# Three FFN heads written out by hand on four engines, in a four-layer trunk on one core

## The chip, the core and the metric

The kernel runs on one core of a Trainium2 chip. A core has TensorE (PE, the matrix engine, with a weight-load side that the profile calls PEld), VectorE (DVE), ScalarE (ACT), GpSimd (POOL) and SyncE (SP, which here only issues DMAs); each takes its instructions from its own queue, in order, and engines wait for each other by semaphores. SBUF is the on-chip memory, PSUM the accumulators of PE. The metric is the device time of one execution, in microseconds (us); lower is better.

## The reference

A trunk of four layers on 512 tokens with D = 1024, everything in float32. Layer by layer the mixer is S5 (a diagonal state-space scan), GLA (gated linear attention), differential attention, and S5 again; behind each mixer stands a SwiGLU feed-forward network with 2816 hidden columns:

```python
for layer in range(DEPTH):
    h = rmsnorm(x, norm_mix[layer])
    mix = s5_mixer | gla_mixer | diff_attn_mixer     # by layer % 3
    x = x + mix
    h = rmsnorm(x, norm_ffn[layer])
    g, u = split(h @ w_gate_up[layer], 2)            # 1024 x 5632
    x = x + (silu(g) * u) @ w_down[layer]            # 2816 x 1024
return rmsnorm(x, norm_final)
```

## The kernel before

**Three matmuls for one.** A float32 operand is split into a high half (rounded to the format fp32r) and the low rest; a product is three matmuls, high x high, high x low, low x high. A split of a weight tile is `halves()`: ACT writes the high half (L235), DVE subtracts it from the weight for the low one (L236). Weights come by `staged()` into a ring of three buffers (`wst`, DMA issued by SP); split weights lie in a ring of five (`whl`).

**Seven products for eight.** The FFNs of layers 1, 2 and 3 (heads 1, 2 and 3 below) use a scheme of Strassen's kind. The left matrix, h transposed, is cut into quarters a11, a12, a21, a22 (tile `halves`, written by `keep`). From them `Sides` makes seven left sides: "11" and "12" are the split quarters themselves; "1" is s = a21 - a22, "2" is s - a11, "4" is s + a12, all three made in place in a21's room; "3" is a11 - a21; "22" is a22. `parts()` splits a side into halves (ACT L154, DVE L155); the totals are L177. The weight columns are cut into 11 blocks of 256 hidden columns; a block needs seven weights, some of them sums, and does seven products (`seven_product`, L458, 24 matmuls of 128x256 each): "one" (side 11), "two" (side 12), "five" (side 1), "six" (side 2), "seven" (side 3), "three" (side 4) and "four" (side 22). "one", "six", "seven" and "four" add up in one PSUM bank, "five" and "three" in a second; "two" has one of its own (PSUM: four banks `acc`, two `s`).

**Where weights lie.** A block's weights "11" and "3" are staged; "21", "1" and "22" lie in rooms (`slots`: three of their own, two lent from a buffer of the activations, and, when the sides are built, the four quarters and the gain's tile). "1" and "3" are sums of two quarters of the weight: SP loads the one, and POOL issues a DMA that adds the other onto it (L485). Within a block W["1"] is then changed twice by a DVE add: plus W["22"] ahead of "six" (L530), plus W["21"] ahead of "four" (L546).

**The norm.** h is x times the gain, without the row's factor. That factor (`finish`: squares on ACT, mean on DVE, the power on POOL, L118) is applied to the products: `rows()` writes four diagonal matrices on DVE (L125), spreads them over the partitions by four matmuls with a matrix of ones on PE (L128, tile `rows`), and ACT copies the result to `R`; `scaled` uses R in `gate1` and `four`.

**The order.** A tile scheduler puts the instructions of each engine into an order, from the program's order, costs and priorities, unless a `manual_schedule` names the engine: then the program's order is kept. In the GLA and the differential-attention mixers PE is kept in program order. At an FFN's head only SP is, for the first loads:

```python
with self.tc.manual_schedule(engines={mybir.EngineType.SP}):
    f[0]["roomed"](None, lent[:, 0])
    f[0]["direct"]()
    f[1]["direct"]()
    f[0]["summed"]()
```

**The tail and the head.** The mixer's last product is `gemm_b` with a `tail`: its last four k-steps run row tile by row tile (t = 0 to 3), so that x is updated (L389), multiplied by the gain (`take`, L83), transposed by PE (`put`, L101) and kept (L158) tile by tile. The differential attention has a loop of its own for that. What I call the head is the part of `ffn()` from there on: block 0's and block 1's first products, the sides, the norm, up to the loop over groups of blocks (4, 4, 3). In that loop a group of blocks is done, and then its part of the down projection.

Of the kernel before, what the change touches and what calls it, by code (L numbers as in the profile page):

```python
# [60 lines left out]
class Left:  # L61
# [4 lines left out]
    def __init__(self, tr, grow, g=None):  # L66
# [10 lines left out]
    def take(self, t, d):  # L77
# [8 lines left out]
        tr.flush(1 - d)  # L86
        tr.pend.append(lambda: self.put(t, d, h))
# [20 lines left out]
    def finish(self):  # L108
# [4 lines left out]
        for t in range(NT):  # L113
            self.square(t, 1)
# [5 lines left out]
    def rows(self):  # L120
        tr = self.tr
        nc = tr.nc
        diag = tr.np_.tile([P, NT, P], F32, tag="h", name="diag")
        for t in range(NT):
            nc.vector.tensor_scalar(diag[:, t], tr.ident[:], self.r[:, t : t + 1], None, op0=ALU.mult)  # L125
        p = tr.tp("rows")
        for t in range(NT):
            nc.tensor.matmul(p[:, t], tr.ones[:], diag[:, t], start=True, stop=True)  # L128
        self.R = tr.np_.tile([P, SEQ], F32, tag="R", name="R", bufs=1)
        nc.scalar.copy(self.R[:].rearrange("p (a b) -> p a b", b=P), p[:])  # L130


class Sides(Left):

    def room(self):
# [3 lines left out]
        self.place = {"11": two[:, 0], "12": two[:, 1]}  # L141

    def open(self, pool):

        for n in ("3", "1", "2", "4", "22"):
            self.place[n] = pool.tile([P, 2, 4, 256], F32R, name="side" + n)
# [14 lines left out]

    def side(self, name):

        v = self.tr.nc.vector
        a11, a12, a21, a22 = (self.F[k] for k in ((0, 0), (0, 1), (1, 0), (1, 1)))
        s = a21
        if name == "22":
            self.parts("22", a22)
        elif name == "3":
            for k in (0, 2):  # L170
                ks = slice(k, k + 2)
                u = self.tr.np_.tile([P, 2, 256], F32, tag="h", name="s3")
                v.tensor_tensor(u[:], a11[:, ks], a21[:, ks], op=ALU.subtract)
                self.parts("3", u[:], ks)
        else:
            x, y, op = {"1": (a21, a22, ALU.subtract), "2": (s, a11, ALU.subtract), "4": (s, a12, ALU.add)}[name]
            v.tensor_tensor(s, x, y, op=op)  # L177
            self.parts(name, s)


class Trunk:
    def __init__(self, ctx, tc, ins, out):
# [23 lines left out]
        self.pend = []  # L206

# [46 lines left out]
    def gemm_b(self, stat, w, nk, c0, evac, k0=0, tail=0, between=()):  # L254
# [53 lines left out]
    def gemm_a4(self, left, hls, banks):  # L308

        for n, (hl, bank) in enumerate(zip(hls, banks)):  # L310
# [4 lines left out]
            if n == 3:  # L315
                left.rows()
# [132 lines left out]
    def seven_product(self, side, w, bank, first):  # L449

        hl = self.halves(w, 4, 256)
# [11 lines left out]
    def seven_block(self, fp, slots, left, wgu, b, turn):  # L463
# [6 lines left out]
        W, bank, keep, lent = {}, {}, {}, set()  # L470

        def load(name, q, half, plus=None, room=None):
            cut = lambda q, half: wgu[
                q * 512 : (q + 1) * 512, half * FFN_HIDDEN + b * 256 : half * FFN_HIDDEN + (b + 1) * 256
            ].rearrange("(a p) n -> p a n", p=P)
            if name in ("11", "3"):
                W[name] = self.staged(cut(q, half), 4, 256)
            else:
# [3 lines left out]
                nc.sync.dma_start(W[name][:], cut(q, half))  # L482
            w = W[name]
            if plus:
                self.added = nc.gpsimd.dma_start(w[:], cut(*plus), accum_op=ALU.add)  # L485
# [22 lines left out]

        def one():
            bank["a"] = self.acc("a")  # L510
            self.seven_product(A["11"], W["11"], bank["a"], True)
# [3 lines left out]
        def two():  # L515
            d = self.sbank("d")
            self.seven_product(A["12"], W["21"], d, True)
            v.tensor_tensor(keep["r1"][:], keep["r1"][:], d[:], op=ALU.add)
# [4 lines left out]
        def five():  # L523
            bank["c"] = self.acc("c")
            self.seven_product(A["1"], W["1"], bank["c"], True)
            keep["r5"] = T("r5")
            nc.scalar.copy(keep["r5"][:], bank["c"][:])

        def six():
            v.tensor_tensor(W["1"][:], W["1"][:], W["22"][:], op=ALU.add)  # L530
            self.seven_product(A["2"], W["1"], bank["a"], False)
# [13 lines left out]
        def four():  # L545
            v.tensor_tensor(W["1"][:], W["1"][:], W["21"][:], op=ALU.add)  # L546
# [20 lines left out]
            direct=direct, roomed=roomed, summed=summed, one=one, two=two, gate1=gate1, five=five, six=six, seven=seven,  # L567
            three=three, four=four,
        )

    def ffn(self, l, left, after=None, turn=False, aside=None):
# [5 lines left out]
        with self.tc.tile_pool(name=f"ffn{l}", bufs=1, reuse_waits="tile") as fp:  # L577
            left.open(fp)
            slots = [fp.tile([P, 4, 256], F32, name=f"slot{n}") for n in range(SLOTS)]
            self.jobs = aside(fp) if aside else iter(())  # L580
# [3 lines left out]
            lent = fp.tile([P, 2, 4, 256], F32, tag="act", name="lent", bufs=4)  # L584
# [11 lines left out]
            left.finish()  # L596
            f[0]["two"]()
            left.side("1")
            f[1]["two"]()
            left.side("2")  # L600
            f[0]["five"]()
            left.rows()
            f[0]["six"]()
            left.side("4")
            left.side("22")
            slots += left.freed() + [left.g[:].rearrange("p (k n) -> p k n", n=256)]
            b0 = 0
            for nb in (4, 4, 3):
                acts = []
                for n in range(b0, b0 + nb):  # L610
# [9 lines left out]
                    todo = ["one", "five", "six", "two", "gate1", "seven", "three"]  # L620
                    if n < 2:
                        todo = ["five", "six", "seven", "gate1", "three"][2 if n == 0 else 0 :]
# [694 lines left out]
    def s5_glu(self, L, zT, accs, after):  # L1317
# [4 lines left out]
        nxt = (Sides if L else Left)(self, after)  # L1322
        with self.tc.tile_pool(name=f"s5g_{L}", bufs=1) as p:
            for d in range(2):
# [18 lines left out]
                self.gemm_b(stat, wg, KT, d * 512, evac_a, tail=4 if d else 0)  # L1343
# [3 lines left out]
    def gla(self, l, left, after):  # L1347
# [4 lines left out]
        with self.tc.tile_pool(name="gla", bufs=1) as p, self.tc.manual_schedule(engines={mybir.EngineType.PE}):  # L1352
# [196 lines left out]
            nxt = Sides(self, after, g)  # L1549
            late = [lambda: turned(1, (0, 1)), lambda: turned(1, (2, 3))]  # L1550
            for d in range(2):
                self.gemm_b(so, wo, KT, d * 512, self.add_x(d, nxt), tail=4 if d else 0, between=late if d == 0 else ())
# [54 lines left out]
    def diff(self, l, left, after):  # L1607
# [3 lines left out]
        with self.tc.tile_pool(name="diff", bufs=1) as p, self.tc.manual_schedule(engines={mybir.EngineType.PE}):  # L1611
            T = lambda tag, bufs=2: p.tile([P, 512], F32, tag=tag, name=tag, bufs=bufs)
            mask = p.tile([P, NT, SEQ], BF16, name="mask")
# [28 lines left out]
            oT = [p.tile([P, 2, 4, SEQ], F32R, name="oT0"), None]  # L1642
# [6 lines left out]
            qks = [None, None]  # L1649
# [16 lines left out]
            def project(hf, z):  # L1666
                if z == 0:
                    qks[hf] = p.tile([P, 2, 4, SEQ], F32, tag="qk", name="qk", bufs=2)
# [150 lines left out]
            def evac0(t, ps):  # L1819
                if not nxt:  # L1820
                    nxt.append(Sides(self, after, gains[0]))
# [49 lines left out]
            run(last)  # L1871
            evac = self.add_x(1, nxt[0])
# [72 lines left out]
```

## Time and profile before

| | |
|---|---|
| three runs | 2402.25, 2408.87, 2411.74 us; median 2408.87 |
| the profiled execution | 2407.16 us, of which its span (the profile's axis) is 2405.4 us |
| busy share of the span | PE 95%, PEld 82%, DVE 62%, ACT 45%, POOL 12% |
| mean granted clock of PE | 0.976 of full speed |

Times in views are microseconds from the span's start. A group's row has its line, engine, operation, output and inputs by the program's names, shapes, and count; then busy time and mean ns of one, and the idle time of that engine just before it with what ended it. A wait's row has the waiting engine and line, what it waited for, the total, the number of times and the longest. In a timeline a row is a start, a length and a group, with the idle time ahead of it in brackets. In a table of windows the columns are length, busy time and count of PE, PEld, DVE, ACT and POOL, PE's granted clock, the share of the DMA engines and GB/s. A row of DMAs has the issuing queue, the count, the size and the time from issue to landing. Matmuls are pipelined, so that the lengths of neighbours overlap.

### The profile page before, as it was taken

What the parts mean: (1) busy time and instruction counts of PE and PEld (TensorE: products, weight loads), DVE (VectorE), ACT (ScalarE), POOL (GpSimd) and SP (SyncE); (2) the same over time, 40 slices, a digit from 0 to 9 for tenths busy, and PEclk for the clock granted to TensorE, in tenths of its full rate; (3) what the DMA queues carried; (4) which work ended last, traced back from release to release, by engine and by line L of the source; (5) the groups of instructions that cost most, each with busy time, mean ns of one, the idle gap of its engine ahead of it and who ended that gap; (6) DMA issues with size and microseconds to landing.
All of it is one profiled execution on the core that took longest, in us unless ns stands there. A gap on an engine that the chain in (4) does not pass through costs nothing. (4 is left out here: it accounts for less than half of the span.)

```text
span 2405.4 us, 35202 instructions
## 1 busy us (share of the span) xinstructions
PE 2276.8 (95%) x14054; PEld 1968.8 (82%) x14054; DVE 1487.2 (62%) x2288; ACT 1071.2 (45%) x1740; POOL 291.9 (12%) x354
## 2 busy tenths in 40 slices
PE   4799999999999989999999998899999799899997
PEld 3578888788877779898987886799998687899996
DVE  7764565555433458585753676776765864867674
ACT  4453435444352345252534675553533223644442
POOL 3330100110100001010001130110000210200000
PEclk9699999999999999999999999999999899899999
DMA  4124343544332348574344564785632643966621
GB/s 110 35 51 140 98 146 133 166 128 161 120 105 71 108 99 214 132 182 125 106 137 114 114 135 137 180 240 133 176 95 72 236 141 100 216 166 150 166 74 67
DMA packets 275503, 317.42 MB, mean 132 GB/s; under 512 B 45653, under 2 KB 214377, under 8 KB 274058
## 3 DMA queue, kind: packets, MB, share of 16 engines
q1 hardware_dynamic: 227210, 238.14, 31.8%
q0 software_dynamic: 48128, 77.02, 15.6%
q8 instruction: 111, 1.82, 0.3%
q14 instruction: 54, 0.44, 0.1%
HBM read 275.92 MB, written 23.99 MB: 125 GB/s over the span
## 5 line engine op out<-in xcount | busy, mean ns | idle before, releaser
L236 DVE TENSOR_TENSOR whl<-wst,whl 128x1024 fp32r<-128x1024 f32 x294 | 359.6, 1225 | 352.3 <-ACT whl L235 351.5
L235 ACT CAST whl<-wst 128x1024 fp32r<-128x1024 f32 x294 | 308.2, 1050 | 519.2 <-PE acc L252 346.6
L458 PE MATMUL a<-side,whl 128*128 128x256 f32 x2376 | 287.7, 277 | 1.6 <-ACT r L533 1.4
L458 PEld LDWEIGHTS a<-side,whl 128*128 128x128 f32 x2376 | 278.1, 188 | 3.1 <-ACT r L533 2.6
L252 PE MATMUL acc<-whl,act 128*128 128x512 f32 x704 | 277.4, 394 | 0.0
L251 PE MATMUL acc<-whl,act 128*128 128x512 f32 x704 | 276.1, 392 | 0.0
L250 PE MATMUL acc<-whl,act 128*128 128x512 f32 x704 | 275.4, 391 | 0.0
L458 PE MATMUL c<-side,whl 128*128 128x256 f32 x1584 | 192.4, 277 | 0.0
L458 PEld LDWEIGHTS c<-side,whl 128*128 128x128 f32 x1584 | 186.2, 188 | 0.0
L251 PEld LDWEIGHTS acc<-whl,act 128*128 128x128 f32 x704 | 132.2, 188 | 29.6
L250 PEld LDWEIGHTS acc<-whl,act 128*128 128x128 f32 x704 | 132.2, 188 | 29.5 <-issue 0.7
L252 PEld LDWEIGHTS acc<-whl,act 128*128 128x128 f32 x704 | 132.3, 188 | 26.8
L250 PE MATMUL any<-hT,whl 128*128 128x512 f32 x384 | 151.7, 395 | 0.0
L251 PE MATMUL any<-hT,whl 128*128 128x512 f32 x384 | 149.6, 390 | 0.0
L252 PE MATMUL any<-hT,whl 128*128 128x512 f32 x384 | 149.6, 390 | 0.0
L250 PE MATMUL acc<-whl,hT 128*128 128x512 f32 x352 | 144.2, 410 | 0.9 <-ACT whl L235 0.6
L251 PE MATMUL acc<-whl,hT 128*128 128x512 f32 x352 | 138.7, 394 | 0.9 <-DVE whl L236 0.9
L252 PE MATMUL acc<-whl,hT 128*128 128x512 f32 x352 | 139.0, 395 | 0.0
L458 PE MATMUL a<-sides,whl 128*128 128x256 f32 x792 | 108.6, 297 | 4.4 <-ACT whl L235 2.6
L458 PEld LDWEIGHTS a<-sides,whl 128*128 128x128 f32 x792 | 105.0, 204 | 6.1 <-ACT whl L235 3.3
L251 PE MATMUL acc<-whl,zT 128*128 128x512 f32 x256 | 103.9, 406 | 5.4 <-DVE whl L236 5.4
L236 DVE TENSOR_TENSOR whl<-halves,whl 128x1024 fp32r<-128x1024 f32 x60 | 73.3, 1223 | 56.0 <-ACT whl L235 56.0
(425 smaller groups left out, 4214.7 us busy)
## 6 DMA issues: line engine op xcount, KB each, us to landing
wst<-in_ffn_w_gate_up_dram SPq DMA_DIRECT2D x110, 512.0 KB, 3.8
wst<-in_ffn_w_down_dram SPq DMA_DIRECT2D x88, 512.0 KB, 4.3
halves<-in_ffn_w_gate_up_dram SPq DMA_DIRECT2D x42, 512.0 KB, 4.8
slot<-in_ffn_w_gate_up_dram SPq DMA_DIRECT2D x39, 512.0 KB, 4.6
wst<-in_ffn_w_gate_up_dram POOLq DMA_DIRECT2D x33, 512.0 KB, 6.2
wst<-in_s_w_glu_dram SPq DMA_DIRECT2D x32, 512.0 KB, 3.7
spill<-opsp POOLq DMA_DIRECT2D x8, 2048.0 KB, 8.7
wst<-in_gla_w_in_dram SPq DMA_DIRECT2D x24, 512.0 KB, 3.6
```

The lines of the kernel that those rows point to most:

```text
L235: nc.scalar.copy(hl[:, 0], w[:])
L236: nc.vector.tensor_tensor(hl[:, 1], w[:], hl[:, 0].bitcast(F32), op=ALU.subtract)
L250: mm(out, lh, rh, start=first, stop=False)
L251: mm(out, lh, rl, start=False, stop=False)
L252: mm(out, ll, rh, start=False, stop=last)
L458: mm(o, hl[:, x, k, c], side[:, y, k], start=first and not (j or k or n), stop=k == 3 and n == 2, skip_group_check=True,)
```

## The change

The stretch from the tail's weights to the end of the head is put into the program's order on PE, ACT, DVE and SP (`hand` opens a manual schedule, `ffn` closes it). In detail:

- `ahead`: the staged weights "11" of blocks 0 and 1 are loaded and split before the tail's row tiles (in the differential attention one ahead of the tail and one ahead of its last row tile). The products take these from `H`; `split` makes the others in the head at the place where the order names it.
- The squares of the second half of the columns are taken by each `take` (`early`), no longer all in `finish`.
- `rows` is cut into `diag` (DVE), `spread` (PE) and `rows` (ACT's copy). The spread now stands behind three products.
- `side` is cut into `total` and `side`. Side 3 is built behind total 2, from s as it is then: s - a11 has become s, and -s - a22 is a11 - a21.
- Products and their evacuations are cut apart (`one`, `one_out` and so on), and block 1's "five" and "six" are part of the head.
- The adds onto W["1"] of blocks 0 and 1 (four for each head) are done by POOL, those of later blocks by DVE as before.
- Rooms in SBUF are opened in another order, where the early splits need room beside the mixer's tiles.

All layers' work outside these three heads, and the counts of matmuls, splits and loads, stay as they were.

```diff
+    def ahead(self, n):
+        E = mybir.EngineType
+        if not self.heads:
+            self.tr.hand(E.PE, E.Activation, E.DVE, E.SP)
+        w = [self.tr.staged(self.quarter(0, 0, b), 4, 256) for b in range(len(self.heads), len(self.heads) + n)]
+        self.heads += [self.tr.halves(y, 4, 256) for y in w]
...
+    def total(self, name):
+        v = self.tr.nc.vector
+        a11, a12, s, a22 = (self.F[k] for k in ((0, 0), (0, 1), (1, 0), (1, 1)))
+        if name == "3":
+            self.us = []
+            for k in (0, 2):
+                u = self.tr.np_.tile([P, 2, 256], F32, tag="h", name="s3")
+                v.scalar_tensor_tensor(u[:], s[:, k : k + 2], -1.0, a22[:, k : k + 2], op0=ALU.mult, op1=ALU.subtract)
+                self.us.append(u)
+        else:
+            y, op = {"1": (a22, ALU.subtract), "2": (a11, ALU.subtract), "4": (a12, ALU.add)}[name]
+            v.tensor_tensor(s, s, y, op=op)
...
+    def hand(self, *engines):
+        if self.guard is not None:
+            self.guard.close()
+        self.guard = ExitStack()
+        if engines:
+            self.guard.enter_context(self.tc.manual_schedule(engines=set(engines)))
...
         if tail:
             hls = [self.wb(w, k0 + kb, c0) for kb in range(nk - tail, nk, 2)]
+            if ahead:
+                ahead()
...
+        def added():
+            (nc.gpsimd if b < 2 else v).tensor_tensor(W["1"][:], W["1"][:], W["22"][:], op=ALU.add)
...
         def four():
-            v.tensor_tensor(W["1"][:], W["1"][:], W["21"][:], op=ALU.add)
+            (nc.gpsimd if b < 2 else v).tensor_tensor(W["1"][:], W["1"][:], W["21"][:], op=ALU.add)
...
-            with self.tc.manual_schedule(engines={mybir.EngineType.SP}):
-                f[0]["roomed"](None, lent[:, 0])
-                f[0]["direct"]()
-                f[1]["direct"]()
-                f[0]["summed"]()
-            f[0]["one"]()
-            left.side("3")
-            f[1]["one"]()
-            self.flush()
+            f[0]["roomed"](None, lent[:, 0])
+            f[0]["summed"]()
             f[1]["roomed"](lent[:, 1], left.g[:].rearrange("p (k n) -> p k n", n=256))
             f[1]["summed"]()
+            f[0]["split"]("21")
+            f[0]["one"]()
             left.finish()
+            f[1]["split"]("21")
+            self.flush()
+            f[1]["one"]()
+            f[0]["one_out"]()
+            left.total("1")
+            left.diag()
+            left.side("1")
+            left.total("2")
+            f[1]["one_out"]()
+            f[0]["split"]("1")
+            left.side("2")
             f[0]["two"]()
-            left.side("1")
+            left.spread()
+            left.rows()
+            f[1]["split"]("1")
             f[1]["two"]()
-            left.side("2")
+            f[0]["two_out"]()
             f[0]["five"]()
-            left.rows()
+            f[0]["added"]()
+            f[0]["split"]("1")
+            f[1]["two_out"]()
+            f[1]["five"]()
+            f[1]["added"]()
+            f[1]["split"]("1")
+            f[0]["five_out"]()
+            left.total("3")
+            left.side("3")
+            f[1]["five_out"]()
             f[0]["six"]()
+            left.total("4")
             left.side("4")
+            f[0]["six_out"]()
+            f[1]["six"]()
             left.side("22")
+            self.hand()
```

More of the change, by code (lines that the diff above doesn't have):

```diff
@@ L86, in take @@
         tr.flush(1 - d)
+        if d and self.early:
+            self.square(t, d)
         tr.pend.append(lambda: self.put(t, d, h))
@@ L112, in finish @@
         v = nc.vector
-        for t in range(NT):
-            self.square(t, 1)
+        if not self.early:
+            for t in range(NT):
+                self.square(t, 1)
         ms = tr.sp.tile([P, NT], F32, tag="ms4", name="ms4", bufs=2)
@@ L566, in seven_block @@
         return dict(
-            direct=direct, roomed=roomed, summed=summed, one=one, two=two, gate1=gate1, five=five, six=six, seven=seven,
-            three=three, four=four,
+            split=split, direct=direct, roomed=roomed, summed=summed, one=one, one_out=one_out, two=two,
+            two_out=two_out, gate1=gate1, five=five, five_out=five_out, added=added, six=six, six_out=six_out,
+            seven=seven, three=three, four=four,
         )
@@ L619, in ffn @@
                             r = self.turn_x(left.r)
-                    todo = ["one", "five", "six", "two", "gate1", "seven", "three"]
+                    todo = ["one", "one_out", "five", "five_out", "added", "six", "six_out", "two", "two_out"]
                     if n < 2:
-                        todo = ["five", "six", "seven", "gate1", "three"][2 if n == 0 else 0 :]
+                        todo = ["six_out"] if n else []
+                    todo += ["gate1", "seven", "three"] if n > 1 else ["seven", "gate1", "three"]
                     for step in todo:
```

130 lines of the change are left out of this document (77 added, 53 removed).

## The prediction

> **What bounds the kernel now.** I read the page first, then the waits of TensorE (PE), then the three heads in the windows and the timeline, and last the groups of the head's VectorE (DVE), ScalarE (ACT) and GpSimd (POOL).
>
> ```profile
> span 2405.4 us, 35202 instructions
> PE 2276.8 (95%) x14054; PEld 1968.8 (82%) x14054; DVE 1487.2 (62%) x2288; ACT 1071.2 (45%) x1740; POOL 291.9 (12%) x354
> ```
>
> PE is busy for 95% of the span, so over the whole kernel only 128.6 us of PE's idle time are there to be won. The waits say how much of it lies at the heads:
>
> ```profile
> PE rows L128 <- DVE diag L125: 11.8, 3, 5.8
> PE tp L101 <- DVE hh L83: 8.1, 7, 1.9
> PE rows L128 <- ACT side L154: 5.0, 1, 5.0
> ```
>
> `rows` is the spreading matmul of the norm, once for each FFN. PE stands there because in its queue the spread comes ahead of the first product, and it needs the norm of all rows. The timeline of PE, head by head (start, length, group):
>
> ```profile
> 878.95 0.40 PE L252 MATMUL acc<-whl,oT 128*128 128x512 f32 x1
> 881.48 0.63 PE L101 MATMUL tp<-ident,hh 128*128 128x128 f32 x4 [1.70 <-DVE hh L83]
> 887.76 0.77 PE L128 MATMUL rows<-diag,ones 128*128 128x128 f32 x2 [5.64 <-DVE diag L125]
> 889.85 8.27 PE L458 MATMUL a<-sides,whl 128*128 128x256 f32 x46 [0.90 <-DVE whl L236]
> ...
> 929.94 2.88 PE L458 MATMUL a<-side,whl 128*128 128x256 f32 x24
> 932.66 3.02 PE L458 MATMUL a<-sides,whl 128*128 128x256 f32 x24
> 935.52 2.67 PE L458 MATMUL c<-side,whl 128*128 128x256 f32 x22
> ...
> 1513.77 0.40 PE L252 MATMUL acc<-whl,oT 128*128 128x512 f32 x1
> 1568.63 3.02 PE L458 MATMUL a<-sides,whl 128*128 128x256 f32 x24
> ...
> 2039.93 0.39 PE L252 MATMUL acc<-whl,zT 128*128 128x512 f32 x1
> 2095.97 3.02 PE L458 MATMUL a<-sides,whl 128*128 128x256 f32 x24
> ```
>
> The mark I use is the end of the 15th product behind the mixer's last matmul (seven of block 0, seven of block 1, "one" of block 2). Head 1 runs from 879.35 to 935.68, 56.3 us; head 2 from 1514.17 to 1571.65, 57.5; head 3 from 2040.32 to 2098.99, 58.7. Undisturbed, a product takes 2.72 us (929.94 to 932.66) or, with the sides "11" and "12", 2.86 (932.66 to 935.52): ten of the first and five of the second are 41.5 us, and with transposes and spread about 43.2. So a perfect head would win 13.1 + 14.3 + 15.5 = 42.9 us, and no more: 2364. The rest of the loss is clock:
>
> ```profile
> 885.00:890.00 5.00, 1.34 (x5) 1.07 (x5) 5.00 (x7) 3.13 (x4) 3.17 (x3) 0.53 0.43 60
> 890.00:895.00 5.00, 5.00 (x24) 5.00 (x25) 4.92 (x6) 2.63 (x4) 0.00 (x0) 0.50 1.18 214
> 900.00:936.00 36.00, 35.82 (x308) 35.23 (x307) 32.50 (x37) 21.04 (x27) 6.41 (x5) 1.00 1.00 229
> ```
>
> In the windows (PE, PEld, DVE, ACT, POOL, clock) PE has full work from 890, but a granted clock of 0.50 until 895: 46 matmuls take 8.27 us where 120 ns each would make 5.5, so 2.8 us are lost behind the gap. From 900 on PE is full, and DVE beside it is at 32.50 of 36 us: DVE is the second limit of this stretch, with hardly a tenth free.
>
> **The change, part by part.** *Splits ahead, rows late.* The two "11" splits go in front of the tail, and the spread goes behind three products. Then PE can start block 0's "one" at 879.6 and needs no norm before about 888.6: on paper the waits of 0.90, 5.64 and part of 1.70 us and the half clock behind them vanish, some 11 us for head 1. In the tail the splits cost nothing, hidden by the tail's 48 matmuls of 128x512 and weights loaded long before; uncovered they would be 2 x 1.05 us on ACT.
>
> ```profile
> L236 DVE TENSOR_TENSOR whl<-wst,whl 128x1024 fp32r<-128x1024 f32 x6 | 7.3, 1220 | 0.1
> L177 DVE TENSOR_TENSOR halves<-halves 128x1024 f32<-128x1024 f32 x3 | 3.7, 1220 | 0.9 <-ACT halves L158 0.9
> L155 DVE TENSOR_TENSOR side<-s,side 128x512 fp32r<-128x512 f32 x2 | 1.4, 685 | 0.0
> L235 ACT CAST whl<-wst 128x1024 fp32r<-128x1024 f32 x6 | 6.3, 1049 | 1.7 <-PE a L458 1.7
> ```
>
> *What DVE must do in the new order.* From the last x add to total "4": nine subtractions of splits and sides, and three totals (128x1024, 1.22 us, about 1.13 back to back), 13.6 us; side 3 in halves (two scaled subtractions and two low halves, some 2.7), two r1 sums, the diag and the norm's small steps, 5.1 together: 18.7 us from 880.7, so 899.4 without a wait. It waits, though, for weights whose second half is added by a DMA:
>
> ```profile
> 886.01 1.34 POOL L485 DMA_DIRECT2D wst<-in_ffn_w_gate_up_dram  x1 [0.50 <-DMA gain<-in_ffn_w_gate_up_dram]
> 886.83 1.83 POOL L485 DMA_DIRECT2D lent<-in_ffn_w_gate_up_dram  x1
> lent<-in_ffn_w_gate_up_dram POOLq DMA_DIRECT2D x1, 512.0 KB, 9.3
> halves<-in_ffn_w_gate_up_dram POOLq DMA_DIRECT2D x1, 512.0 KB, 9.0
> wst<-in_ffn_w_gate_up_dram POOLq DMA_DIRECT2D x4, 512.0 KB, 6.8
> ```
>
> Block 1's "1" keeps its place in POOL's queue behind block 0's two and the norm's power: issued near 886 and landing 6.8 to 9.3 us later, at 893 to 896. In the hand order its split stands in DVE's and ACT's queue ahead of all that follows, so f1's "five" starts near 896.2, 1.4 to 2.3 us after PE is free for it (894.8), and r1's first sum, the two second splits, side 3 and total 4 are queued behind it.
>
> *The four adds of a head go to POOL.* W1 += W22 and W1 += W21 of blocks 0 and 1 are 128x1024 adds, 1.22 us on DVE (as L177 above). On POOL:
>
> ```profile
> 19.52 2.35 POOL L352 TENSOR_TENSOR scr<-sq,gain 128x1024 f32<-128x1024 f32 x1 [1.67 <-ACT sq L350]
> 19.64 2.33 DVE L756 TENSOR_TENSOR params<-params 128x64 f32<-128x64 f32 x1
> L756 DVE TENSOR_TENSOR params<-params x3: 206/213/2330, 9.6 to 22.2; 128x64 f32<-128x64 f32 x3
> 1900.35 1.27 POOL L1127 TENSOR_TENSOR mods<-mods 128x512 f32<-128x512 f32 x1 [5.93 <-DVE mods L1125]
> 1901.57 2.19 POOL L1128 TENSOR_TENSOR mods<-mods 128x512 f32<-128x512 f32 x1
> 1900.79 1.91 DVE L1137 TENSOR_TENSOR_SCAN mods<-cs,mods 128x512 f32<-128x512 f32 x1
> 1902.62 2.23 DVE L1139 TENSOR_TENSOR_SCAN mods<-cs,mods 128x512 f32<-128x512 f32 x1
> ```
>
> An add of this size takes 2.35 us there, and it isn't beside DVE: L756, 0.21 us by its median, took 2.33 when it met L352, and ended with it; near 1900 scans and POOL adds stretch each other in turn. Both read two operands from SBUF, as do all splits, totals and sides. [...] I take the former, less where DVE idles anyway: the first (about 891.6 to 894) falls into DVE's wait for block 1's "1" and is free; the other three each push DVE by 2.35, where 1.22 had stood. Total 4 comes at 910.6 (905.7 with the three free), and side 3's low half near 908 to 909. On PE "six" ends at 906.2, so "seven" waits about 3.3 us.
>
> *Side 3 from the sum* adds no operation (two scaled subtractions for two plain ones, 0.75 for 0.69 us at most) but puts side 3 behind total 2 and the splits: part of that 3.3 us.
>
> *What is late next: block 2.* Its "1" is loaded into the quarter a12, which total 4 reads last; before, that total was done early:
>
> ```profile
> 897.66 1.22 DVE L177 TENSOR_TENSOR halves<-halves 128x1024 f32<-128x1024 f32 x1
> ```
>
> So the room is free at 910.6, not 898.88. Load about 6.4 us (the busy queue), then an accumulating DMA third in POOL's queue, about 9 us with issue, then ACT 1.05 and DVE 1.22: ready at 928.3. In heads 1 and 3 PE's new order puts two matmuls of block 2's "five" ahead of block 1's "seven" and "four"; PE reaches them near 923.8 and would idle 4.5 us, then has 8.2 us of the fifteen left: 936.6. In head 2 "seven" stands ahead of them and covers 2.7 of it.
>
> **The sum.** Head 1: 936.6 against 935.7, +0.9, and a clock that drops once behind the 3.3 or the 4.5 us stop, +1 (a third of the 2.8 above, as not each stop need do so): +1.9. Head 2: the same chain from its tail is 57.3, less 2.7 for the order, and with the shorter stop (1.8 us) I leave the 1 us for the clock out: 54.6 against 57.5, -2.9. Head 3: 57.3 + 1 = 58.3 against 58.7, and its first accumulation is no longer behind the power, some 0.5 less (half of the power's 1.0): -0.9. Together -1.9 us. Elsewhere the order of work is the same. The profiled execution took 2407.16 us (span 2405.4 and 1.76 around it), 1.7 below the median of 2408.87: 2407.2 - 1.9 = 2405.3, so **2405 us**. What moves this: an add's price on DVE between -1.2 (no lock) and 2.35, that is -4.9 to +9.4 us a head; block 2's "1" between 923 and 932.
>
> **Rivals.** (a) *The cover holds.* POOL's adds find DVE's idle places, total 4 is done at 905.7, block 2's "1" at 923.4, nothing waits: the fifteen end at 931.7, 52.3 us a head. Gains 4.0 + 5.2 + 6.4 = 15.6: 2391.6. For it: PE is up to 10 us ahead at the start; against it: 32.50 of 36 us. Chance 0.26. (b) *Nearly the ceiling*, three quarters of 42.9: 2375. It would need DVE's 28 us of work and locks under PE's first 23. 0.07. (c) *Slower: block 2's "1" late at half clock.* Accumulations queue behind each other; if this one lands 3.7 us later, at 932 ready, PE idles 8 us, more than the 5.64 after which the clock was 0.50, and the next 46 matmuls cost 2.8 more: 943, +7.3 in head 1, +5.5 in head 3 and +3 in head 2, with no gain left: +16, 2423. It decides from about 930 on. [...] 0.17. (d) *It does not do what it says*: the adds, the rows and the heads trade places, but DVE is full either way and the fifteen end where they did: 2407, 0.05. My forecast keeps 0.45, with 2398 to 2413 as its own range.
>
> **How the numbers follow.** 0.5% is 12 us, about what a measurement of this kernel can tell from no change: faster is below 2397, slower above 2421. Faster takes (a) but for a little, and (b): 0.32. Slower takes most of (c) and a trace of the forecast: 0.18. Same is the forecast and (d), with the edges: 0.50. The range runs from 2385 to 2424: it leaves out (b), the lower end of (a) and the upper of (c), about 0.17.
>
> **What would show it.** Right: the waits of the spread for diag are gone, the first three or four products run without a gap at clock 1.00 from 879.6; twelve POOL adds of 128x1024 of 2.3 us or more, and DVE rows beside them that are stretched to 3 us and more; new waits of PE for side 3 or its split near the ninth product, and for block 2's "1". Wrong, towards faster: those waits under 1 us each, and DVE rows at 1.22 beside POOL's adds. Wrong, towards slower: windows of clock 0.50 in the second half of the heads, or a tail that grew because ACT's and DVE's early splits hold up its evacuations.

## The result, and the profile after

The changed kernel took 2432.77 us (median of 4 runs, 2430.78 to 2434.80) against 2406.61 for the kernel before in the same comparison (2402.25 to 2411.74): 1.0108 times as long, 95% interval 1.0084 to 1.0132. That is slower by 26 us, where the forecast was no change, and outside its range. The profiled execution took 2430.78 us, its span is 2428.7, 23.3 above that of before.

First the page of the changed kernel, then PE's waits:

```profile
span 2428.7 us, 35189 instructions
PE 2281.9 (94%) x14054; PEld 1975.6 (81%) x14054; DVE 1490.2 (61%) x2276; ACT 1071.3 (44%) x1740; POOL 328.9 (14%) x366
```

```profile
PE a L505 <- ACT r L595: 26.5, 4, 9.7
PE c L505 <- ACT whl L276: 13.6, 5, 4.1
PE tp L106 <- DVE hh L86: 4.0, 3, 2.2
```

The waits of the spread for the diag (11.8 and 5.0 us) are gone, as forecast. Two new ones have taken their place. L505 is the matmul of a product, L595 ACT's copy of a block's bank a behind "six" (`six_out`), L276 the cast of a split. They lie in the heads; here is PE in head 1:

```profile
874.87 0.40 PE L293 MATMUL acc<-whl,oT 128*128 128x512 f32 x1
875.46 3.12 PE L505 MATMUL a<-sides,whl 128*128 128x256 f32 x24
878.77 3.11 PE L505 MATMUL a<-sides,whl 128*128 128x256 f32 x24
885.41 3.12 PE L505 MATMUL d<-sides,whl 128*128 128x256 f32 x24
888.37 2.90 PE L505 MATMUL c<-side,whl 128*128 128x256 f32 x24
892.45 0.50 PE L505 MATMUL c<-side,whl 128*128 128x256 f32 x2 [1.18 <-ACT whl L276]
893.71 4.40 PE L505 MATMUL c<-side,whl 128*128 128x256 f32 x22 [0.76 <-DVE whl L277]
909.27 5.49 PE L505 MATMUL a<-side,whl 128*128 128x256 f32 x24 [5.59 <-ACT r L595]
927.28 0.50 PE L505 MATMUL c<-side,whl 128*128 128x256 f32 x2 [3.92 <-ACT whl L276]
934.58 3.00 PE L505 MATMUL a<-side,whl 128*128 128x256 f32 x24
```

Both "one" products are done 6.6 us behind the tail (881.88 from 875.27); before it was 18.8 (898.12 from 879.35). So 12.2 us are won, and then 18.1 are lost: the fifteenth product ends at 937.58, 62.3 us behind the tail against 56.3. Three stops, the first of them in two parts (1.18 and 0.76), make 1.94 + 5.59 + 3.92 = 11.45 of the 18.1. The clock makes most of the rest; the same stretch in windows (the eighth column is the granted clock):

```profile
875.00:892.00 17.00, 16.27 (x138) 15.98 (x136) 11.40 (x16) 8.82 (x13) 9.20 (x5) 1.00 0.87 193
892.00:898.00 6.00, 4.79 (x25) 4.59 (x26) 5.57 (x5) 3.20 (x5) 3.10 (x2) 0.72 0.37 67
898.00:908.00 10.00, 5.68 (x49) 5.48 (x48) 10.00 (x8) 5.51 (x8) 4.92 (x3) 1.00 0.43 133
908.00:915.00 7.00, 5.73 (x27) 5.73 (x28) 5.00 (x6) 3.76 (x6) 3.42 (x3) 0.51 0.95 209
928.00:932.00 4.00, 4.00 (x24) 4.00 (x23) 4.00 (x6) 1.10 (x2) 1.33 (x2) 0.59 0.30 97
```

Each stop is followed by a stretch of lowered clock, in which PE is at work: 4.79 x 0.28 + 5.73 x 0.49 + 4.00 x 0.41 = some 5.8 us of work lost.

The single executions differ by some us in stretches that no edit touches (the changed kernel's tail in head 1 ends 4.1 us earlier than before's, behind the same instructions). So the experiments are read by the length of each head, from the end of the mixer's last matmul to the end of the 28th product (four blocks), taken from PE's timeline. From there to the end of the last block's products every FFN takes the same 223.9 us, but for the three kernels noted.

| | head 1 | head 2 | head 3 | median, us | ratio to before (95%) |
|---|---|---|---|---|---|
| before | 92.2 | 93.4 | 94.5 | 2407 to 2408 | 1 |
| changed | 97.9 | 107.5 | 98.2 | 2432.8 | 1.0108 (1.0084 to 1.0132) |
| e1_adds_dve | 94.1 | 107.6 | 94.1 | 2429.6 | 1.0095 (1.0075 to 1.0115) |
| e2_six_out | 97.8 | 106.0 | 99.5 | 2433.9 | 1.0110 (1.0091 to 1.0129) |
| e3_rooms | 94.7 | 108.0 | 95.8 | 2429.6 | 1.0098 (1.0076 to 1.0120) |
| e4_both | 92.5 | 102.4 | 93.2 | 2417.9 | 1.0048 (1.0032 to 1.0064) |
| e5_both_dve | 88.9 | 98.8 | 89.5 | 2411.6 | 1.0014 (1.0000 to 1.0029) |
| e6_turn_later | 92.0 | 93.6 + 9.0 later | 93.3 | 2419.9 | 1.0051 (1.0036 to 1.0067) |
| e7_all | 84.2 | 87.7 + 7.8 later | 84.8 | 2392.2 | 0.9937 (0.9912 to 0.9962) |
| e8_sched_act_dve | 94.6 | 104.7 | 92.2 | 2423.7 | 1.0067 (1.0051 to 1.0084) |
| e9_turn_early | 84.2 | 92.3 | 84.8 | 2396.4 | 0.9945 (0.9924 to 0.9965) |
| e10_early_sum | 96.2 | 108.0 | 94.7 | 2428.1 | 1.0093 (1.0057 to 1.0128) |
| e11_all_pool_adds | 90.4 | 89.2 + 8.7 later | 91.1 | 2411.7 | 1.0016 (1.0005 to 1.0028) |
| e12_diff_ahead_late | 84.2 | 93.2 | 84.8 | 2386.6 | 0.9911 (0.9892 to 0.9929) |
| e13_turn_block2 | 84.4 | 93.8 | 84.8 | 2388.0 | 0.9929 (0.9905 to 0.9953) |
| e14_after_no_turn | 98.4 | 98.2 | 98.3 | 2424.4 | 1.0082 (1.0067 to 1.0097) |
| e15_before_no_turn | 92.0 | 92.2 | 93.9 | 2405.0 | 0.9995 (0.9984 to 1.0005) |
| e16_after_diff_late | 98.9 | 109.8 | 98.5 | 2432.8 | 1.0116 (1.0097 to 1.0135) |

"Later" is what the FFN loses beyond the 223.9 us, by one wait in the first down projection (5.7 to 5.9 us) and the clock behind it (in e6 the first matmul behind the wait takes 0.80 us; behind a stop of 0.95 us at clock 1.00, at 1286.90 before, such a one takes 0.50). The turn in the names is explained with e6.

### The profile page after: what moved, and what is told of

Its sections match the earlier page's. It is cut to its first block, busy times and chain, and to the rows that moved or that the text cites. A ratio compares the mean times of both kernels' runs of the same rounds, so it can differ in the third digit from the quotient of the medians.

```text
span 2428.7 us, 35189 instructions
## 1 busy us (share of the span) xinstructions
PE 2281.9 (94%) x14054; PEld 1975.6 (81%) x14054; DVE 1490.2 (61%) x2276; ACT 1071.3 (44%) x1740; POOL 328.9 (14%) x366
## 5 line engine op out<-in xcount | busy, mean ns | idle before, releaser
L276 ACT CAST whl<-wst 128x1024 fp32r<-128x1024 f32 x294 | 308.3, 1050 | 526.2 <-PE acc L293 351.5
L505 PE MATMUL a<-side,whl 128*128 128x256 f32 x2376 | 298.9, 284 | 26.5 <-ACT r L595 26.5
L505 PEld LDWEIGHTS a<-side,whl 128*128 128x128 f32 x2376 | 289.9, 195 | 27.4 <-ACT r L595 27.3
L505 PE MATMUL c<-side,whl 128*128 128x256 f32 x1584 | 198.5, 282 | 15.8 <-ACT whl L276 13.6
L505 PEld LDWEIGHTS c<-side,whl 128*128 128x128 f32 x1584 | 191.5, 193 | 17.4 <-ACT whl L276 14.6
L277 DVE TENSOR_TENSOR whl<-slot,whl 128x1024 fp32r<-128x1024 f32 x63 | 82.4, 1309 | 46.8 <-ACT whl L276 46.8
L292 PE MATMUL acc<-whl,zT 128*128 128x512 f32 x256 | 104.1, 407 | 5.5 <-DVE whl L277 5.5
L291 PE MATMUL acc<-whl,zT 128*128 128x512 f32 x256 | 103.2, 406 | 2.7 <-ACT zT L407 2.7
```

The costliest lines, as they stand in the source:

```text
L276: nc.scalar.copy(hl[:, 0], w[:])
L277: nc.vector.tensor_tensor(hl[:, 1], w[:], hl[:, 0].bitcast(F32), op=ALU.subtract)
L291: mm(out, lh, rh, start=first, stop=False)
L292: mm(out, lh, rl, start=False, stop=False)
L505: mm(o, hl[:, x, k, c], side[:, y, k], start=first and not (j or k or n), stop=k == 3 and n == 2, skip_group_check=True,)
```

## The experiments

**Who holds what.** The queue that PE waits for in head 1 is ACT's. ACT, POOL and DVE of the changed kernel around the long stop:

```profile
907.69 1.04 ACT L182 CAST side<-halves 128x1024 fp32r<-128x1024 f32 x1 [0.48 <-DVE halves L202]
908.64 0.58 ACT L595 COPY r<-a 128x512 f32<-128x512 f32 x1
...
897.28 2.40 POOL L608 TENSOR_TENSOR slot<-slot,slot 128x1024 f32<-128x1024 f32 x1 [1.16 <-DVE whl L277]
900.85 2.78 POOL L608 TENSOR_TENSOR lent<-lent,slot 128x1024 f32<-128x1024 f32 x1 [1.16 <-DVE whl L277]
913.34 1.30 POOL L534 DMA_DIRECT2D halves<-in_ffn_w_gate_up_dram  x1 [1.09 <-DMA halves<-in_ffn_w_gate_up_dram]
...
892.43 1.23 DVE L277 TENSOR_TENSOR whl<-lent,whl 128x1024 fp32r<-128x1024 f32 x1 [4.79 <-ACT whl L276]
897.13 0.67 DVE L574 TENSOR_TENSOR r<-r,d 128x512 f32<-128x512 f32 x1
897.73 3.04 DVE L277 TENSOR_TENSOR whl<-lent,whl 128x1024 fp32r<-128x1024 f32 x1
900.69 3.48 DVE L198 SCALAR_TENSOR_TENSOR s<-halves 128x512 f32<-128x512 f32 x2
906.44 1.21 DVE L202 TENSOR_TENSOR halves<-halves 128x1024 f32<-128x1024 f32 x1
```

"Six" of block 0 was done near 901, but its copy L595 stands behind side 4's cast (L182), which waits for total 4 (L202, 906.44), which DVE does behind rows that POOL's adds stretch to 3.04 and 3.48 us. "Seven" adds onto the same bank, so PE waits for the copy. Theories: Q, positions in queues (this copy, and the late room of block 2's "1"); L, the stretched DVE rows are the cause.

**e1_adds_dve** gives both adds of blocks 0 and 1 (of W["22"] and of W["21"]) back to DVE; the line below stands for the two.

```diff
-(nc.gpsimd if b < 2 else v).tensor_tensor(W["1"][:], ...)
+v.tensor_tensor(W["1"][:], ...)
```

> The changed kernel with one part undone: the four adds onto W1 of each head are DVE's again. Theory Q (queues): the loss comes from two places in queues, ACT's copy of block 0's bank a (line 595) behind side 4's cast, and block 2's weight '1', whose room, load and accumulating DMA come late; the adds on POOL only feed the first. DVE then does 4 x 1.22 us itself where its rows beside POOL's adds were stretched by 1.8 us each, and the split behind each add waits for ACT in between, so total 4 comes 1 to 2 us earlier a head: 2425 to 2431 us, waits for L595 of 3.5 to 5 us remain in each head. Rival L (lock): the stretched DVE rows are the cause, directly and through total 4: without them each head is 5 us or more shorter, 2412 to 2417 us, waits for L595 under 1 us.

2429.6 us: Q's figure, not L's. Heads 1 and 3 are 4 us shorter, head 2 isn't. A stop of 3.7 us remains at the same place in each head (it is now block 0's "three" that waits for side 4's cast; PE's order moved with the edit), and a wait for L595 of 6.3 us in head 2.

**e2_six_out, e3_rooms and e4_both**

```diff
             f[0]["six"]()
+            f[0]["six_out"]()
             left.total("4")
             left.side("4")
-            f[0]["six_out"]()
             f[1]["six"]()
+            f[1]["six_out"]()
...
-                        todo = ["six_out"] if n else []
+                        todo = []
```

> The changed kernel with ACT's copy of bank a behind 'six' moved directly behind 'six' for block 0 (ahead of total 4 and side 4) and for block 1 (into the head's written order). Theory Q: block 0's 'seven' no longer waits for side 4's cast but for side 3's low half, which is 2.8 us earlier in head 1 (906.44 against 909.27), about the same in the others, with half a us to 1 us of clock; in head 2 block 1's 'seven' no longer waits behind the cast of block 2's '1', some 3.4 us: together 12 to 17 us, 2416 to 2421 us. Rival L: the place of the copy is nothing, DVE's late side 3 and total 4 hold PE as long: within 4 us of the changed kernel, 2429 to 2433.

```diff
-        return [self.F[k] for k in ((0, 0), (0, 1), (1, 0), (1, 1))]
+        return [self.F[k] for k in ((0, 1), (0, 0), (1, 0), (1, 1))]
```

> The changed kernel with block 2's weights '21' and '1' exchanged between the quarters a11 and a12: the '1', which needs a load and an accumulating DMA behind it, gets a11, which is free after total 2 (about 885 in head 1) and not after total 4 (907.6). Theory Q: the waits for its cast near the end of the heads go (3.9, 9.7 and 4.1 us) with the clock that drops behind them (1.5 us each): 16 to 22 us, 2411 to 2417 us; the three waits of 5.6 us for L595 stay. Rival C (contention): the DMAs are slow because the queues are full in this stretch, an earlier start moves the accumulation before block 1's own '1', which then comes later: gain under 8 us, 2425 or more, and a longer wait at block 1's 'five'.

> e2_six_out and e3_rooms together. Theory Q: both effects add up except for the 3.4 us of head 2 that both count: 25 to 33 us less than the changed kernel, 2400 to 2408 us, about the kernel before or a little below. Rival L: only the part of the rooms is there, 2411 to 2417 us, with PE still waiting 4 us or more ahead of block 0's 'seven' in each head.

e2 missed: 2433.9 us, nothing won. The stop ahead of "seven" shrank to 3.13 us as expected, but PE then stood 5.43 us ahead of block 1's last product, and 12.3 in head 2, for the bank that a DVE row behind block 2's late "1" frees:

```profile
913.43 4.64 PE L505 MATMUL a<-side,whl 128*128 128x256 f32 x24 [3.13 <-ACT r L595]
937.98 2.29 PE L505 MATMUL a<-side,whl 128*128 128x256 f32 x9 [5.43 <-DVE r L599]
```

e3, 2429.6 us, won 3.2 of the 16 to 22 us expected. Block 2's "1" is in time, but the 5.2 us for side 4 remain (in its place PE waits ahead of "three"), and in head 2 a stop of 9.5 us comes 83 us behind the tail. e4 has both, 2417.9 us: 15 us less where its parts alone won 3 and lost 1, so each wait had been covered by the other. It is still 10 us above what Q expected at most: heads 1 and 3 are level with before, head 2 is 9.0 us longer. Q isn't all.

**e5_both_dve** is e4 with e1's edit.

> e4_both with the four adds of each head back on DVE. In e4_both two r x R multiplies stand beside POOL's adds for 6.58 us in head 1 and two scaled subtractions for 3.48, where alone they take about 1.3 and 1.5; PE waits 2.5 and 1.1 us behind them (more in heads 2 and 3). Theory L (the lock is a real part of the loss, once the queues are mended): those waits shrink to about 1 us together, 2 to 3 us a head: 2408 to 2413 us. Theory Q alone (queues are all): within 2 us of e4_both, 2416 to 2420.

2411.6 us, L's figure: each head is 3.6 or 3.7 us shorter. (That makes 10.9 us by the heads of the profiled executions; the medians differ by 6.3, and e5's ten executions run from 2402 to 2417 us, the profiled one being the fastest.) Here is what POOL's adds did to DVE in head 1 of e4, and the same groups in e5; L543 multiplies by `R`, L198 is the scaled subtraction of side 3:

```profile
L543 DVE TENSOR_TENSOR r<-r,R 128x512 f32<-128x512 f32 x2 | 6.6, 3328 | 0.0
L198 DVE SCALAR_TENSOR_TENSOR s<-halves 128x512 f32<-128x512 f32 x2 | 3.5, 1779 | 0.0
```

```profile
L543 DVE TENSOR_TENSOR r<-r,R 128x512 f32<-128x512 f32 x2 | 1.4, 685 | 0.0
L198 DVE SCALAR_TENSOR_TENSOR s<-halves 128x512 f32<-128x512 f32 x2 | 1.3, 688 | 0.0
```

**e6_turn_later.** In layer 2 the FFN also turns x (a copy of 2 MB to DRAM and back, `turn_x`), issued by POOL behind block 2's loads.

```diff
-                    if turn and n == 2:
+                    if turn and n == 3:
```

> e4_both with the turn of x in layer 2 (a 2 MB copy out and back, issued by POOL behind block 2's loads) issued behind block 3's loads. Theory T (the turn's DMAs delay the accumulating DMAs of blocks 2 and 3, which come late in the new order): head 2, 102.4 us to the end of the 28th product in e4_both against 93.4 before, falls to 93 to 96, the waits of 2.5 and 5.2 us near its end go: 2409 to 2413 us, heads 1 and 3 as in e4_both. Rival: block 3's weights are late because their rooms come free late: head 2 stays at 100 or more, 2415 to 2420.

2419.9 us, a miss by the time and a hit by the place: head 2 falls to 93.6, but the cost only moves (93.6 + 9.0 against 102.4). The down projection now stands 5.9 us, behind a DVE row that frees its bank. That row is queued behind the split of a down weight, and ACT waits 7.43 us for this weight's load:

```profile
1623.21 0.80 PE L291 MATMUL acc<-whl,act 128*128 128x512 f32 x1 [5.91 <-DVE g L543]
1620.30 1.23 DVE L277 TENSOR_TENSOR whl<-wst,whl 128x1024 fp32r<-128x1024 f32 x1 [5.67 <-ACT whl L276]
1619.22 1.04 ACT L276 CAST whl<-wst 128x1024 fp32r<-128x1024 f32 x1 [7.43 <-DMA wst<-in_ffn_w_down_dram]
```

**e7_all** adds to e5 and e6 that POOL is in the written order, and a later "3" of block 1:

```diff
-            self.tr.hand(E.PE, E.Activation, E.DVE, E.SP)
+            self.tr.hand(E.PE, E.Activation, E.DVE, E.SP, E.Pool)
...
-            f[1]["summed"]()
             f[0]["split"]("21")
             f[0]["one"]()
             left.finish()
+            f[1]["summed"]()
```

> e5_both_dve and e6_turn_later together, and POOL in the written order too, with block 1's weight '3' loaded behind finish: so block 1's '1' is accumulated before the norm's power and not behind it. If Q, L and T hold and add up, the wait of block 1's 'five' (2.1 us in head 1) goes with the clock behind it, and the heads come to 88 to 90 us, head 2 to 92 against 92.2, 93.4 and 94.5 before: 2398 to 2404 us, below the kernel before. If the gains don't add up (another late weight takes the place of each wait): 2408 or more.

2392.2 us, below the range, and faster than before by 0.6%. Heads 1 and 3 fall by 4.7 from e5; PE waits at most 0.9 us at a time in head 1:

```profile
PE a L505 <- DVE whl L277: 0.9, 1, 0.9
PE a L505 <- ACT r L595: 0.8, 1, 0.8
PE c L505 <- DVE side L183: 0.7, 1, 0.7
```

**e8_sched_act_dve** leaves ACT and DVE to the scheduler again (`hand(E.PE, E.SP)`).

> The changed kernel with the written order for PE and SP alone: ACT and DVE are ordered by the scheduler again. Theory Q: the scheduler may put ACT's copy of bank a where it is ready, so that the waits for L595 fall from 5.6 us to 2 or less, while block 2's late '1' stays: 2418 to 2426 us. Rival O (a written order is better than the scheduler's, and only its details are wrong): side 3 and the splits come in a worse order, waits ahead of PE's written products grow: 2435 us or more.

2423.7 us, as Q expected. The written order of these two engines costs 9 us as it stands, but e7's written order is 31 us better than the scheduler's here; that comparison has the other edits in it too.

**e10_early_sum** has the two edits of this diff alone (POOL in the written order, the later "3"), on the changed kernel.

> The changed kernel with POOL in the written order too and block 1's '3' loaded behind finish, nothing else: block 1's '1' is accumulated before the norm's power. Its rooms, its copies of bank a, its adds on POOL and the turn stay. Theory W (that late weight is a root: its split stands in DVE's and ACT's queues 4.8 us idle in front of all the rest of the head): the first wait (1.9 us in head 1) goes, and total 4, side 4 and with them the wait for L595 and block 2's '1' come 4 to 5 us earlier: 10 to 16 us, 2417 to 2423 us. Rival Q alone: the first wait goes, but PE then comes to the wait for L595 earlier and stands there longer: 2428 to 2433.

2428.1 us: the rival, at the edge of its range, though the four executions spread from 2423 to 2441 us. The first stop is gone, and PE comes 3 us earlier to the same wait:

```profile
905.74 5.42 PE L505 MATMUL a<-side,whl 128*128 128x256 f32 x24 [5.66 <-ACT r L595]
```

**e11_all_pool_adds** is e7 with the adds on POOL.

> e7_all with the four adds of each head on POOL, as in the changed kernel: the price of the lock alone, in a head in which the queues are mended. From e4_both to e5_both_dve the heads lost 3.6, 3.6 and 3.7 us of length without the lock. Theory L: the same comes back: 10 to 12 us, 2401 to 2405 us, DVE rows beside the adds at 3 us and more. Rival: with block 1's '1' early DVE has slack, and the lock falls into it: 2391 to 2396.

2411.7 us: 19.5 more than e7, nearly twice what was expected. The rows are stretched as in e4 (two L543 in 6.3 us), head 1 is 6.2 longer and head 3 6.3, and PE stops there for 3.0 us; the profile's mean granted clock is 0.977 against e7's 0.983. The profiled executions are 19.3 us apart, of which the three FFNs make 14.9; the rest lies in stretches that the edit doesn't touch. So with the queues mended, the place of these adds alone decides whether the order gains 0.6% or nothing (1.0016).

**e9_turn_early, e12_diff_ahead_late and e13_turn_block2**: e7 with the turn at the head's end (`n == 0`); with the early splits of the differential attention's tail moved as well; and e12 with the turn back at `n == 2`.

```diff
             run(last)
-            nxt[0].ahead(1)
...
                 banks.append(self.acc())
-                if t == 3:
-                    nxt[0].ahead(1)
+                nxt[0].ahead(1)
```

> e7_all with the turn of x in layer 2 issued at the end of the head, ahead of the DMAs that add onto block 2's weights, not behind block 3's. In e7_all head 2 has lost 11.3 us against head 1 by the end of the FFN (319.35 against 308.07), 5.7 of it in a wait of the down projection for the turned x or row factors. Theory T: copied early, beside loads that have 25 us of slack, the turn delays nothing: head 2 comes to 85 us at the 28th product and 308 to 310 at the end, 2381 to 2385 us. Rival: 4 MB of copies slow the accumulations of block 2 as they did in the changed kernel, or hold those queued behind the copy back on POOL: 2390 or more, with a new wait for block 2's '1' or '3'.

> e9_turn_early with the differential attention's two early splits ahead of its third and fourth row tile, not ahead of the first and fourth. In the changed kernel the tail of that mixer is 2.8 us longer than before, with waits of 1.0 and 2.2 us of PE's transposes for the gain's multiply, which stands behind the first split in DVE's queue. If that is so: 1 to 3 us below e9_turn_early, and these waits under 0.7 us. Rival: the waits are there for the tail's own order, unchanged: within 1 us of e9_turn_early.

> e12_diff_ahead_late with the turn of x behind block 2's loads, its place in both kernels of the case. With the turn at the head's end (e12) head 2 lost 9 us against the others, by a wait of 5.9 us for block 2's weights; behind block 3 (e7) 11.3 us by the end of the FFN. Theory T2 (wherever the turn stands in this fast order, its 4 MB cost the accumulating DMAs behind it): 317 to 319 us at the end of head 2's FFN, 2385 to 2389 us. Rival: behind block 2 is the gap that the kernel before found: 310 to 312 us there, 2379 to 2382 us.

e9, 2396.4 us, is the rival: a new wait of 5.5 us for block 2's weights. e12 is the best kernel of the study, 2386.6 us, 0.9% below before. It won 9.8 us where 1 to 3 were expected; the tail's waits of 1.04 and 2.16 us are gone, and with them a stretch of half clock (the profile's mean is 0.983 against 0.982). The profiled executions are 7.6 us apart. PE's last 97 instructions in that tail take 25.3 us in e9 and 19.7 in e12: 5.6 us are the tail's. In every run with the first placement they take 22.6 to 25.3 us, in all three with the later one 19.7. Another 2.8 us lie ahead of the tail in that layer, in work that the edit doesn't touch and that takes from 296 to 303 us over the executions of this study. e13, 2388.0, agrees with T2: behind block 0, 2 or 3 the turn costs this order 8 to 11 us, measured against its heads 1 and 3. No run has this order without the turn.

**e14_after_no_turn and e15_before_no_turn** leave the turn out (`if False:`), so that the layers behind it work on rows in the wrong order.

> The changed kernel without the turn of x in layer 2 (its four DMAs are left out, so the last layers compute on rows in the wrong order). Theory T (of head 2's 14 us the part beyond the other heads' 4 to 6 is the turn's): head 2's FFN falls from 331.4 to 322 to 323 us, as in heads 1 and 3, and the wait of 9.7 us to 4: 2421 to 2425 us. Rival: block 2's '1' is late in head 2 whatever else is moved: 2428 us or more.

> The kernel before without the turn of x (the same left out): what the turn costs where its copy finds a gap. Theory T: 1 to 2 us, the 1.2 us wait of head 2: 2404 to 2407 us. Rival: the turn always costs some 9 us: 2398.

2424.4 and 2405.0 us. In the changed kernel head 2 becomes like the others (98.2 from 107.5); before, it loses 1.2 us. So 9 of head 2's 14 us are the turn's.

**e16_after_diff_late** is e12's edit alone on the changed kernel.

> The changed kernel with the differential attention's two early splits ahead of its third and fourth row tile, nothing else. From e9 to e12 this won 9.8 us by the medians, of which the traces show 3.2 us of waits and a window of half clock. If that is the edit's own: 5 to 9 us, 2424 to 2428 us, no wait of the transposes there. Rival: in the changed kernel the tail's wait is hidden by what comes behind it (head 2 waits for weights anyway): 2431 to 2434 us.

2432.8 us, the same as without. The tail's waits are gone, and the tail is 5.5 us shorter (19.7 against 25.2). Heads 2 and 1 give 2.3 and 1.0 us of that back (109.8 and 98.9). The profiled execution also reaches head 1 3.9 us later than the changed kernel's, ahead of every edit. So what the edit is worth in the median isn't shown.

## Why the prediction was wrong, step by step

**Right.** The gain at the start: 12.2 us against "some 11". The first stop: f1's "five" was to wait 1.4 to 2.3 us, it waited 1.94, at the place and for the weight named. The room of block 2's "1" and the order of PE in heads 1 and 3. The four adds and their rows: three pushes of up to 2.35 us were priced, in head 1 two splits grew by 1.8 each and two scaled subtractions by 2.1 together, 5.7 in all. (Two of its sums here don't come out: three pushes of 2.35 are 7.05, where its two figures for total 4, 905.7 and 910.6, are 4.9 apart, and side 3 at 908 to 909 behind "six" at 906.2 is a wait of 1.8 to 2.8, not 3.3.) That an add pushes DVE by the 2.35 us that the sum takes for each of three, no row of this head shows: beside adds of 2.38, 2.40 and 2.78 us the pushes were these 1.8, 1.8 and 2.1. Nor did every row beside an add grow: L183 at 886.41 (both inputs in SBUF) and L574 at 897.13 (one in PSUM), which began just ahead of the adds at 886.52 and 897.28, took 1.23 and 0.67 us, and the split behind L574 3.04. Without POOL's adds, in e5, the three take 1.23, 0.68 and 1.22.

**Failed: "'seven' waits about 3.3 us".** The chain was walked on DVE and PE and not on ACT. Block 0's copy of bank a stands in ACT's written order behind side 4's cast, so that "seven" waited for total 4 and not only for side 3: in head 1 it starts 34.0 us behind the tail, not 30.2, and the stop is 5.59, 5.67 and 5.52 us in the three heads. The prediction's own total 4, done at 910.6, with a cast of 1.05 and a copy of 0.58 us behind it, gives 912.2 and a stop of 6.0 us. e2 and e4 show the place: alone it wins nothing, with the rooms mended 11.7 us (2429.6 to 2417.9).

**Mis-sized: block 2's "1" in head 1.** Nine us were taken for the accumulating DMA with its issue; it was 12.9 in head 1 (913.34 to the cast at 926.19).

**Failed: head 2, "'seven' stands ahead of them and covers 2.7 of it".** Block 1's copy of bank a is behind block 2's cast in ACT's queue, so "seven" itself waited, 9.72 us. And the turn wasn't priced: the late room lets POOL issue it first.

```profile
1557.57 1.30 POOL L734 DMA_DIRECT2D xturn<-vall  x1
1558.67 1.53 POOL L534 DMA_DIRECT2D halves<-in_ffn_w_gate_up_dram  x1
1578.87 1.04 ACT L276 CAST whl<-halves 128x1024 fp32r<-128x1024 f32 x1 [10.98 <-DMA halves<-in_ffn_w_gate_up_dram]
1581.39 5.49 PE L505 MATMUL a<-side,whl 128*128 128x256 f32 x24 [9.72 <-ACT r L595]
```

The accumulation is ready 20.2 us behind its issue. The order of POOL's queue was there to be read before; the prediction moved the weight behind other loads and never asked what else was in that queue. Forecast -2.9 us, measured +14.1, of which 9.3 go with the turn.

**Failed: "In the tail the splits cost nothing".** This held in heads 1 and 3, whose tails are as long as before. In the differential attention's tail the first early split stands in ACT's and DVE's queues among the row tiles' work. The same transposes on PE wait 1.04 and 2.16 us for the multiply by the gain where they waited 0.34 and 1.01, and a stretch of half clock follows (0.51 from 1505.5 to 1509). The last 97 instructions take 25.2 us where they took 22.4:

```profile
1501.46 1.41 PE L106 MATMUL tp<-ident,hh 128*128 128x128 f32 x8 [1.04 <-DVE hh L86]
1505.73 1.09 PE L106 MATMUL tp<-ident,hh 128*128 128x128 f32 x4 [2.16 <-DVE hh L86]
```

**Mis-sized: the clock.** One us in heads 1 and 3 and none in head 2, against 5.8 in head 1. Both of its signs of "wrong, towards slower", windows of clock 0.50 late in the heads and a tail that grew, are there.

**The balance.** To the 28th product the heads lost 5.7 + 14.1 + 3.7 = 23.5 us; the tail of the differential attention is 2.8 us longer. That is 26.3, against 26.2 by the medians; in the profiled executions a start 4.1 us earlier hides part of it. The forecast was -1.9. Rival (c), block 2's "1" late at half clock with 2423 us and a chance of 0.17, came nearest by its time and not by its mechanism: its stop was 3.9 and 4.1 us in heads 1 and 3, nearer the forecast's own 4.5 than its 8, and there were two more that it didn't have.

**What stays open.** The parts don't add: e2 and e3 win -1 and 3 alone and 15 together, the adds 3 in the changed kernel, 6 from e4 to e5 and 19.5 in the mended one. That each wait covers the next is shown by the waits. The 2.8 us ahead of the tail in e12 have no cause here. Whether the turn holds block 2's "1" up by its place in POOL's queue or by its traffic isn't shown: e14 takes away both at once.

## What to carry to other kernels

When an order is written by hand for several in-order engines, walk every queue, the evacuating engine's too: an evacuation that frees an accumulator must not stand behind work that waits for another engine. Give rooms that come free late to weights that are needed late and are loaded in one step, and look at what else the queue of an accumulating DMA holds. Adds moved to GpSimd to relieve VectorE can cost VectorE more than doing them: here 5.7 us of stretched rows in head 1 against 4.9 for the four adds (4 x 1.22).

## What the runs showed of the hardware

In the changed kernel's head 1, stops of 1.18 and 0.76 us with two matmuls between them were followed by a stretch of lowered clock (0.72 over 892 to 898). Behind the stops of 0.87, 0.83 and 0.74 us in e7's head 1, 22, 24 and 46 matmuls took 2.77, 3.01 and 5.63 us, 0.12 to 0.13 us each, as undisturbed, and over e12's head 1 (876 to 925) the clock is 1.00. Nor does the same stop have the same sequel each time: in the differential attention the profile of before (at 1286.90) and that of the changed kernel (at 1288.49) have the same stop, 0.95 and 0.96 us for the same split, and one of 0.61 us a matmul ahead of it. Behind them the clock was 0.50 in the one (1289 to 1291; a 128x512 matmul took 0.63 us) and 1.00 in the other (1290 to 1293; 0.39 us). So the length of a stop alone doesn't tell. The mean granted clock of e12's profile is 0.983 against 0.976 before.

The norm's power on POOL, 128x4, took 1.93 us in the changed kernel's head 1, where it began while a split of DVE was running. It took 1.02 before, where none was running when it began:

```profile
879.52 1.93 POOL L124 TENSOR_TENSOR rcol<-ms,mhalf 128x4 f32<-128x4 f32 x1 [30.03 <-DVE ms L123]
879.33 1.22 DVE L277 TENSOR_TENSOR whl<-slot,whl 128x1024 fp32r<-128x1024 f32 x1
```
